# A gated delta-rule block on one core: key and query tiles by turns, decay summed in place, byte masks, shared scan banks, one joined product, and weights rounded on GpSimd

## The chip, the cores and the metric

The kernel runs on one core of a Trainium2 chip. The time is the device time of one execution in microseconds (us). Three runs of the kernel before gave 2235.35, 2230.29 and 2233.08 us, so the median is 2233.08 us.

The engines are named as the profile names them: PE (TensorE, matmuls), PEld (its weight loads), DVE (VectorE), ACT (ScalarE), POOL (GpSimd) and SP (the queue that issues nearly all DMAs). Each works through its instructions in the program's order; a scheduler fixes that order when the program is built.

## What is computed

One layer of a diffusion block over 2048 latent and 256 context tokens of width 1024. One projection feeds two branches: a gated delta rule in chunks (branch A) and a gated linear recurrence (branch B), each scanned forwards and backwards. Both are normalized, gated, projected and merged. The part of branch A that the change touches:

```python
def gdn_chunk_scan(q, k, v, g, beta, s0):
    ...
    G = jnp.cumsum(g, axis=-1)
    diff = G[..., :, None] - G[..., None, :]
    decay = jnp.where(incl, jnp.exp(jnp.where(incl, diff, 0.0)), 0.0)
    kb = k * beta[..., None]
    a_mat = jnp.where(strict, jnp.einsum('bhncd,bhnsd->bhncs', kb, k) * decay, 0.0)
    ...
    sol = lax.linalg.triangular_solve(a_mat + eye, rhs, left_side=True, lower=True,
                                      unit_diagonal=True)
    w, u = sol[..., :dk], sol[..., dk:]
    attn = jnp.einsum('bhncd,bhnsd->bhncs', q, k) * decay
    ...
    def step(S, inp):
        w_c, u_c, qg_c, attn_c, kd_c, gl_c = inp
        v_new = u_c - jnp.einsum('bhcd,bhdv->bhcv', w_c, S)
        o_c = jnp.einsum('bhcd,bhdv->bhcv', qg_c, S) + jnp.einsum('bhcs,bhsv->bhcv', attn_c, v_new)
        S = S * gl_c[..., None, None] + jnp.einsum('bhcd,bhcv->bhdv', kd_c, v_new)
        return S, o_c
```

The kernel works in chunks of 128 tokens (18 of them: 2 of context, 16 latent), with 4 heads of 128.

## The kernel before

The stages follow each other, and the scheduler lets them overlap:

1. Inputs are normalized and turned; the projections of branch A run with their convolutions; then branch B is scanned.
2. **prep** (L761) handles one chunk of branch A for both directions. It loads `l`, the chunk's keys, queries and values in one tile of one buffer. It transposes keys, queries and values (`pk`, `pq`, `pv`), sums their squares on ACT, and forms the products key by key (`pkk`, L814) and key by query (`pkq`, L822). For each direction `d` a row of log decays is loaded into `gb` (L802, two buffers), summed along the row on DVE into `dec` (L806, two buffers), put through exp on ACT (L808) and masked on POOL (L810). DVE multiplies it into `pkk` to give `an` (L817) and into `pkq` in place (L824); that result leaves through `atN` (L825). The blocks of `an` leave through `anD` and `dgD`.
3. **solve** (L837) inverts the 32x32 diagonal blocks of four chunks at once, in 62 dependent DVE instructions (L850 and L852 by turns). **levels** (L857) puts a chunk's inverse together from small PE products named `lvt`.
4. **stepA** (L959) is the scan: 18 steps in each direction, each a chain of PE products `psA`, DVE work (`r` at L991, `S` at L998) and scaled copies on ACT (L985: `vx`, `vv`, `o`).
5. The merge and the output projection end the program.

Beside stages 2 to 4 run the **gate projections**: L217, L218 and L219 by turns, 24 matmuls of 512 columns for one block of 128 output features and one group of 512 tokens. They wait for little, so the scheduler puts them between the other PE work. Below, "a filler" is one of these matmuls. Their weights come by `w_part` (L199): a DMA into `ws` (one buffer, L202), a rounding to `wh` on ACT (L203), and the remainder `wl` on POOL (L204).

In PSUM, the pool `pc` has three banks under the tag `t`, taken by turns by `pk`, `pq`, `pv`, `pkk` and `pkq`. The pool `pd` has two banks for the scan's `psA`; it is open during prep, which doesn't use it.

## Time and profile before

| what | us |
|---|---|
| median of three runs | 2233.08 |
| the profiled execution | 2233.26 |
| its span, first to last instruction | 2231.6 |

The page's part 5 groups instructions: line, engine, operation, what is written and read, count, then busy time and the mean ns of one, then the engine's idle time ahead of them and what ended it. A view of windows gives the busy time of each engine in a stretch of the span, with the number of instructions in brackets. A row of the timeline has the start and the duration, and in square brackets the idle time ahead of the instruction and what ended it. Busy times on PE are latencies that overlap: 24 fillers in a row start about 0.23 us apart and take 0.39 us each.

### The profile page before, as it was taken

What the parts mean: (1) busy time and instruction counts of PE and PEld (TensorE: products, weight loads), DVE (VectorE), ACT (ScalarE), POOL (GpSimd) and SP (SyncE); (2) the same over time, 40 slices, a digit from 0 to 9 for tenths busy, and PEclk for the clock granted to TensorE, in tenths of its full rate; (3) what the DMA queues carried; (4) which work ended last, traced back from release to release, by engine and by line L of the source; (5) the groups of instructions that cost most, each with busy time, mean ns of one, the idle gap of its engine ahead of it and who ended that gap; (6) DMA issues with size and microseconds to landing.
All of it is one profiled execution on the core that took longest, in us unless ns stands there. A gap on an engine that the chain in (4) does not pass through costs nothing. (4 is left out here: it accounts for less than half of the span.)

```text
span 2231.6 us, 40198 instructions
## 1 busy us (share of the span) xinstructions
PE 2114.9 (95%) x15056; PEld 1767.6 (79%) x15056; DVE 1404.9 (63%) x3225; ACT 925.3 (41%) x2334; POOL 688.2 (31%) x672
## 2 busy tenths in 40 slices
PE   8999999999999999999998988999989888999998
PEld 3778888888888888888776776788778877888887
DVE  4826666727776777786588788733332348766665
ACT  4623222224443444443455554344453354444441
POOL 3413433412222323234333332221133224433331
PEclk9999999999999999999999999999999999999999
DMA  9312222223323433336777778776888864444432
GB/s 340 110 35 76 64 71 77 83 76 95 106 87 100 126 95 104 101 104 195 219 224 225 255 241 214 228 231 208 236 276 278 258 228 147 145 136 127 142 95 80
DMA packets 308277, 348.15 MB, mean 156 GB/s; under 512 B 78635, under 2 KB 218161, under 8 KB 308083
## 3 DMA queue, kind: packets, MB, share of 16 engines
q1 hardware_dynamic: 306067, 338.26, 49.1%
q0 software_dynamic: 2016, 7.34, 0.9%
q8 instruction: 118, 1.93, 0.4%
q14 instruction: 76, 0.62, 0.1%
HBM read 230.46 MB, written 115.06 MB: 155 GB/s over the span
## 5 line engine op out<-in xcount | busy, mean ns | idle before, releaser
L217 PE MATMUL ps<-uhi,wh 128*128 128x512 f32 (+1 forms) x1824 | 708.2, 388 | 2.9 <-DVE uhi L306 2.6
L218 PE MATMUL ps<-ulo,wh 128*128 128x512 f32 (+1 forms) x1824 | 707.6, 388 | 3.4 <-POOL ulo L311 1.7
L219 PE MATMUL ps<-uhi,wl 128*128 128x512 f32 (+1 forms) x1824 | 705.3, 387 | 0.0
L218 PEld LDWEIGHTS ps<-ulo,wh 128*128 128x128 f32 x1824 | 345.9, 190 | 66.7 <-POOL ulo L311 2.8
L217 PEld LDWEIGHTS ps<-uhi,wh 128*128 128x128 f32 x1824 | 345.7, 190 | 66.4 <-DVE uhi L306 3.9
L219 PEld LDWEIGHTS ps<-uhi,wl 128*128 128x128 f32 x1824 | 345.6, 189 | 62.1 <-POOL wl L204 0.4
L204 POOL TENSOR_TENSOR wl<-ws,wh 128x512 fp32r<-128x512 f32 x144 | 200.2, 1391 | 551.7 <-ACT wh L203 494.4
L203 ACT CAST wh<-ws 128x512 fp32r<-128x512 f32 x144 | 89.4, 621 | 309.5 <-DMA ws<-in_w_in_dram 213.9
L419 DVE SCALAR_TENSOR_TENSOR acc<-raw,cols,acc 128x512 f32<-128x512 f32 x192 | 152.8, 848 | 0.9
L1143 PE MATMUL py<-yh,wab 128*128 128x256 f32 x512 | 145.9, 286 | 5.8 <-DVE mg L1146 5.4
L1144 PE MATMUL py<-yl,wab 128*128 128x256 f32 x512 | 145.1, 284 | 1.3 <-POOL yl L1126 1.3
L1145 PE MATMUL py<-yh,wab 128*128 128x256 f32 x512 | 144.6, 283 | 0.0
L1162 PE MATMUL pso<-uhi,mh 128*128 128x512 f32 x256 | 102.6, 402 | 7.8 <-ACT mh L1148 4.7
L605 POOL TENSOR_TENSOR bg<-s,fz 128x512 f32<-128x512 f32 (+1 forms) x36 | 37.8, 1049 | 224.9 <-ACT X L585 86.7
L1143 PEld LDWEIGHTS py<-yh,wab 128*128 128x128 f32 x512 | 97.7, 191 | 8.0 <-DVE mg L1146 6.6
L1164 PE MATMUL pso<-uhi,ml 128*128 128x512 f32 x256 | 102.2, 399 | 0.6 <-DVE ml L1149 0.6
L1163 PE MATMUL pso<-ulo,mh 128*128 128x512 f32 x256 | 101.8, 398 | 0.0
L1144 PEld LDWEIGHTS py<-yl,wab 128*128 128x128 f32 x512 | 97.7, 191 | 2.1 <-POOL yl L1126 1.7
L1145 PEld LDWEIGHTS py<-yh,wab 128*128 128x128 f32 x512 | 98.7, 193 | 0.2
L1126 POOL TENSOR_TENSOR yl<-gt,yh 128x512 fp32r<-128x512 f32 x32 | 45.0, 1408 | 148.3 <-ACT yh L1125 148.3
L998 DVE SCALAR_TENSOR_TENSOR S<-S,gl,psA 128x128 f32<-128x128 f32 x136 | 38.3, 342 | 82.5 <-PE psA L979 82.4
L1136 ACT ACTIVATE mg<-mg 128x512 f32<-128x512 f32 x64 | 40.4, 632 | 113.0 <-DMA mg<-gT 110.4
(374 smaller groups left out, 3942.3 us busy)
## 6 DMA issues: line engine op xcount, KB each, us to landing
ws<-in_w_in_dram SPq DMA_DIRECT2D x144, 256.0 KB, 3.4
gT<-gt SPq DMA_DIRECT2D x96, 256.0 KB, 3.6
kv<-knvD SPq DMA_DIRECT2D x36, 512.0 KB, 5.1
kq<-qkvD SPq DMA_DIRECT2D x32, 512.0 KB, 6.0
an<-atN SPq DMA_DIRECT2D x32, 512.0 KB, 6.2
mg<-gT SPq DMA_DIRECT2D x64, 256.0 KB, 3.4
qkvD<-acc SPq DMA_DIRECT2D x48, 256.0 KB, 2.3
l<-qkvD SPq DMA_DIRECT2D x16, 768.0 KB, 6.5
```

Of the source, the lines that this page charges most:

```text
L203: ac.copy(out=wh[:, j:j + 4, :], in_=ws)
L204: po.tensor_tensor(out=wl[:, j:j + 4, :], in0=ws, in1=wh[:, j:j + 4, :].bitcast(F32), op=ALU.subtract)
L217: te.matmul(out=ps, lhsT=wh[:, k, :], rhs=uhi[gi][:, k, :], start=(k == 0), stop=False)
L218: te.matmul(out=ps, lhsT=wh[:, k, :], rhs=ulo[gi][:, k, :], start=False, stop=False)
L219: te.matmul(out=ps, lhsT=wl[:, k, :], rhs=uhi[gi][:, k, :], start=False, stop=(k == KB - 1))
L419: ve.scalar_tensor_tensor(out=a_, in0=raw[:, o + k:o + k + n], scalar=wk, in1=a_, op0=ALU.mult, op1=ALU.add)
L1143: te.matmul(out=py[:, i, :], lhsT=wh[:, k, ms_], rhs=yh[i][:, k, :], start=(k == 0), stop=False)
L1144: te.matmul(out=py[:, i, :], lhsT=wh[:, k, ms_], rhs=yl[i][:, k, :], start=False, stop=False)
L1145: te.matmul(out=py[:, i, :], lhsT=wl[:, k, ms_], rhs=yh[i][:, k, :], start=False, stop=(k == H - 1))
L1162: te.matmul(out=ps, lhsT=mh[:, k, ts_], rhs=wout[0][k][:, ns], start=(k == 0), stop=False)
L1163: te.matmul(out=ps, lhsT=mh[:, k, ts_], rhs=wout[1][k][:, ns], start=False, stop=False)
L1164: te.matmul(out=ps, lhsT=ml[:, k, ts_], rhs=wout[0][k][:, ns], start=False, stop=(k == KB - 1))
```

## The change

- **Byte masks.** The four triangular masks are kept for the whole program as bytes (`tri8`) and no longer as five 128x128 tiles of 4 bytes a value. Where they feed a product of branch A's decays they are built again, and the tile of ones is replaced by two masks that add up to it: four more matmuls of 72 columns.
- **Keys and queries by turns.** `l` has two buffers and holds keys and queries; values have a tile of their own, `vT`.
- **Decay summed in place.** The row of log decays is loaded into `dec` itself, and the sum overwrites it; `gb` is gone. `dec` has three buffers, two of them used by each chunk.
- **Scan's banks.** `pq` and `pv` take the two banks of `pd`.
- **Joined product.** One product of the keys with keys and queries side by side (256 columns) for each head, in two banks of two heads each, in place of `pkk` and `pkq`. DVE's multiplication into the decay becomes four of 256 columns in place of two of 512.
- **Weights rounded on GpSimd.** From prep on, `wh` (80 instructions) and the weights of the merge (16) are rounded on POOL, ahead of the subtraction there.

```diff
+    tri8 = cp.tile([P, 4, P], U8, name="tri8")
...
+    with tc.tile_pool(name="tri", reuse_waits="tile", bufs=1, side="right") as tri:
+        for i, t in enumerate(tris(tri, ones)):
+            ve.tensor_copy(out=tri8[:, i, :], in_=t.bitcast(F32))
...
+    hi_ = [ac.copy]
...
-        ac.copy(out=wh[:, j:j + 4, :], in_=ws)
+        hi_[0](out=wh[:, j:j + 4, :], in_=ws)
         po.tensor_tensor(out=wl[:, j:j + 4, :], in0=ws, in1=wh[:, j:j + 4, :].bitcast(F32), op=ALU.subtract)
...
-        for masks, dst in (((m_le, m_ge), eG), ((m_gt, m_lt), erem), ((onesr, onesr), gl)):
+        for masks, dst in ((((m_le,), (m_ge,)), eG), (((m_gt,), (m_lt,)), erem), (((m_le, m_gt), (m_ge, m_lt)), gl)):
...
+    hi_[0] = po.tensor_copy
...
-            l = rc.tile([P, 3, H, P], F32, tag="l", name="l", bufs=1)
-            if lat:
-                sy.dma_start(out=l, in_=qkvD[ch])
-            else:
-                sy.dma_start(out=l[:, 0:3:2], in_=qkvD[ch, :, 0:3:2])
-            kT, qT, vT = l[:, 0], l[:, 1], l[:, 2]
+            l = rc.tile([P, 2, H, P], F32, tag="l", name="l")
+            vT = rc.tile([P, H, P], F32, tag="vT", name="vT", bufs=1)
+            sy.dma_start(out=l[:, 0:1 + lat], in_=qkvD[ch, :, 0:1 + lat])
+            sy.dma_start(out=vT, in_=qkvD[ch, :, 2])
+            kT, qT = l[:, 0], l[:, 1]
...
-                pq = pc.tile([P, H, P], F32, tag="t", name="pq", bufs=3)
+                pq = pd.tile([P, H, P], F32, tag="A", name="pq")
...
-            pv = pc.tile([P, H, P], F32, tag="t", name="pv", bufs=3)
+            pv = pd.tile([P, H, P], F32, tag="A", name="pv")
...
-                gb = rc.tile([P, H * P], F32, tag="gm", name="gb")
-                sy.dma_start(out=gb, in_=gD[d, ch].rearrange("h t -> (h t)").partition_broadcast(P))
-                dc = rc.tile([P, H, P], F32, tag="dec", name="dec")
+                dc = rc.tile([P, H, P], F32, tag="dec", name="dec", bufs=3)
+                row = dc.rearrange("p h t -> p (h t)")
+                sy.dma_start(out=row, in_=gD[d, ch].rearrange("h t -> (h t)").partition_broadcast(P))
...
+            nq = 2 if lat else 1
+            pks = [pc.tile([P, 2, 2, P], F32, tag="t", name="pkk", bufs=3) for _ in range(2)]
             for h in range(H):
-                te.matmul(out=pkk[:, h, :], lhsT=kT[:, h, :], rhs=kT[:, h, :], start=True, stop=True)
...
+                te.matmul(out=pks[h // 2][:, h % 2, 0:nq, :], lhsT=kT[:, h, :], rhs=l[:, 0:nq, h, :], start=True, stop=True)
...
-                pkq = pc.tile([P, H, P], F32, tag="t", name="pkq", bufs=3)
-                for h in range(H):
-                    te.matmul(out=pkq[:, h, :], lhsT=kT[:, h, :], rhs=qT[:, h, :], start=True, stop=True)
                 for d in range(2):
-                    ve.tensor_tensor(out=dec[d], in0=pkq, in1=dec[d], op=ALU.mult)
+                    for hh in range(2):
+                        own = dec[d][:, 2 * hh:2 * hh + 2, :]
+                        ve.tensor_tensor(out=own, in0=pks[hh][:, :, 1, :], in1=own, op=ALU.mult)
                     sy.dma_start(out=atN[ch, :, d, 0], in_=dec[d])
...
-            ac.copy(out=hi[:, k, n:n + 512], in_=ws)
+            hi_[0](out=hi[:, k, n:n + 512], in_=ws)
```

The scheduler orders the program anew. Up to the end of branch B's scan PE's order stays the same but for the four products more; the order differs from there to the end of stage 4.

**PE, in prep.** The rows below are of one latent chunk in the kernel before, ahead of and behind its two products; `ps` rows are fillers.

```order
L219 MATMUL ps<-uhi_434,wl 128x512
L814 MATMUL pkk<-l 128x128 x4
L822 MATMUL pkq<-l 128x128 x4
L217 MATMUL ps<-uhi_434,wh 128x512
L218 MATMUL ps<-ulo_435,wh 128x512
```

In the changed kernel the same place reads:

```order
L224 MATMUL ps<-ulo_333,wh 128x512
L825 MATMUL pkk<-l 128x256 x2
L225 MATMUL ps<-uhi_332,wl 128x512
L791 MATMUL pq<-ident,l 128x128 x4
L223 MATMUL ps<-uhi_332,wh 128x512
L224 MATMUL ps<-ulo_333,wh 128x512
L802 MATMUL pv<-ident,vT 128x128 x4
L825 MATMUL pkk<-l 128x256 x2
L784 MATMUL pk<-ident,l 128x128 x4
L225 MATMUL ps<-uhi_332,wl 128x512
```

The products stand in two pairs of heads with fillers and the next chunk's transposes between them; from the first chunk's products to the last chunk's, the order before has 898 fillers and the changed one 570. The fillers left over stand behind prep: the first product of the scan that waits for `r` comes after 928 and 910 fillers.

**DVE, in prep.** The rows are of the kernel before, from one chunk's `an` to the next chunk's two sums (L806).

```order
L817 SCALAR_TENSOR_TENSOR an<-pkk,nbz,dec 128x128 x8
L824 TENSOR_TENSOR dec<-pkq,dec 128x512
L830 COPY pk__10696<-an 64x4x64
L833 STREAM_TRANSPOSE dg<-an 32x128 x4
L878 COPY yt<-lvt 128x4x32
L824 TENSOR_TENSOR dec<-pkq,dec 128x512
L830 COPY pk__10696<-an 64x4x64
L806 SCALAR_TENSOR_TENSOR dec<-gb,after_9962 128x512
L806 SCALAR_TENSOR_TENSOR dec<-gb,after_9963 128x512
L885 COPY N_9955<-lvt 32x4x32 x2
```

In the changed kernel, from one chunk's last `an` on (`sT` and `sX` are solve's):

```order
L829 SCALAR_TENSOR_TENSOR an<-pkk,nbz,dec 128x128 x4
L835 TENSOR_TENSOR dec<-pkk,dec 128x256 x2
L815 SCALAR_TENSOR_TENSOR dec<-dec,after_9978 128x512
L861 TENSOR_TENSOR sT<-sA,sX 128x240
L835 TENSOR_TENSOR dec<-pkk,dec 128x256 x2
L841 COPY pk__10702<-an 64x4x64
L796 RECIPROCAL sk<-sk 128x4
L803 TENSOR_TENSOR kv<-pv,nk 128x512
L863 TENSOR_TENSOR sX<-sX,sT 128x12x20
L797 SCALAR_TENSOR_TENSOR nbz<-beta,sk 128x2x4
L861 TENSOR_TENSOR sT<-sA,sX 128x231
L799 TENSOR_TENSOR nbze<-nbz,erem 128x2x4
```

The sum of one direction now stands between the two multiplications into `dec`, and the other direction's follows some 20 rows behind the first multiplication (not shown). Between the first and the last `an`, the order before has 211 of solve's rows and the changed one 154; the rest of them now stand behind the last `an` and, all but for levels, ahead of the scan's first `r`.

**SP, in prep.** The rows are DMA issues of the kernel before, from one chunk's `atN` to the loads of `gb`. In brackets stands what an issue waits for; names with DMAHW are landings of earlier DMAs.

```order
L825 DMA atN<-dec 128x512 [waits DVE_49]
L835 DMA dgD<-dg 128x8x32 [waits DMAHW5_49,DVE_49,Activation_49]
L825 DMA atN<-dec 128x512 [waits DMAHW6_49,DVE_49]
L831 DMA anD<-pk__10429 128x384 [waits DMAHW7_49,DVE_49]
L233 DMA gT<-gt 128x512 [waits DVE_49]
L202 DMA ws<-in_w_in_dram 128x4x128 [waits DMAHW3_49,DMAHW1_49,Pool_49]
L802 DMA gb<-gD 128x512 [waits DMAHW2_49,DVE_49]
L802 DMA gb<-gD 128x512 [waits DVE_49]
L795 DMA knvD<-kv 128x1024 [waits DMAHW4_49,DVE_49,Activation_49]
```

In the changed kernel, from one chunk's `atN` to the two loads of `dec`:

```order
L836 DMA atN<-dec 128x512 [waits DVE_49]
L846 DMA dgD<-dg 128x8x32 [waits DMAHW0_49,Activation_49]
L836 DMA atN<-dec 128x512 [waits DMAHW1_49,DVE_49,Pool_49]
L842 DMA anD<-pk__10528 128x384 [waits DMAHW2_49,DVE_49]
L812 DMA dec<-gD 128x512 [waits DMAHW7_49,DMAHW3_49]
L804 DMA knvD<-kv 128x1024 [waits DMAHW4_49,DVE_49]
L239 DMA gT<-gt 128x512 [waits DMAHW5_49,DVE_49]
L812 DMA dec<-gD 128x512 [waits DMAHW6_49,DMAHW1_49]
L208 DMA ws<-in_w_in_dram 128x4x128 [waits Pool_49]
L239 DMA gT<-gt 128x512 [waits DMAHW0_49,Activation_49]
```

The load of the decay row waited for DVE's sum, which frees `gb`. It now waits for landings, among them that of the `atN` transfer out of the buffer it writes, and it stands on the queue ahead of the next loads of weights.

## The prediction

> **What bounds the kernel now.** I read the span and the busy shares first, then the busy times by stretch, then who PE waited for.

> ```profile
> span 2231.6 us, 40198 instructions
> PE 2114.9 (95%) x15056; PEld 1767.6 (79%) x15056; DVE 1404.9 (63%) x3225; ACT 925.3 (41%) x2334; POOL 688.2 (31%) x672
> ...
> core 0: us, PE busy (x) PEld busy (x) DVE busy (x) ACT busy (x) POOL busy (x), PEclk, DMA share, GB/s
> ...
> 1039.50:1179.50 140.00, 127.42 (x727) 105.78 (x725) 98.41 (x259) 70.83 (x242) 47.73 (x49) 1.00 0.75 231
> 1179.50:1359.20 179.70, 160.21 (x1307) 129.06 (x1308) 152.62 (x405) 97.67 (x334) 59.04 (x74) 0.96 0.79 240
> 1359.20:1388.00 28.80, 22.85 (x206) 18.66 (x204) 23.40 (x64) 8.13 (x28) 5.29 (x6) 0.99 0.68 167
> 1388.00:1797.90 409.90, 382.09 (x3368) 329.26 (x3369) 160.82 (x485) 179.55 (x569) 99.10 (x113) 0.98 0.79 246
> 1797.90:2231.60 433.70, 406.90 (x2530) 360.52 (x2529) 274.36 (x452) 175.59 (x476) 143.44 (x97) 0.98 0.42 134
> ```

> PE is busy 95% of the span. Its work hardly changes, so the time can move only by PE's idle time. The first two windows are prep, from the first chunk's `pkk` to the eighth's (1179.5) and to the last one's (1359.2): 319.7 us, PE busy 287.6, idle 32.1. The third runs to the scan's first `r` product, the fourth is the rest of the scan, the last the merge, whose code doesn't change but for who rounds its weights. In prep DVE is busy 251.0 us, 79%.

> ```profile
> PE psA L979 <- ACT vx L985: 12.5, 8, 2.9
> PE pkk L814 <- ACT kv L778: 9.2, 9, 1.5
> PE pkq L822 <- ACT junk L784: 8.0, 9, 2.8
> PE psA L979 <- DVE r L991: 7.8, 2, 4.9
> PE pkq L822 <- DVE kv L794: 6.1, 5, 1.7
> PE pk L775 <- DMA l<-qkvD: 5.5, 4, 1.9
> ```

> Columns are the total in us, the number of waits and the longest. The waits of `pkk`, `pkq` and `pk` sum to 28.8 us, most of prep's 32.1. The first two products wait for a bank: with three banks by turns, `pkk` needs the one that `pk` held until ACT had copied it, `pkq` that of `pq` or `pv`. `pk` waits for the load into the single buffer of `l`.

> **What the change removes.** With `pq` and `pv` in the scan's two banks, and `l` in two buffers, each of these four waits loses its cause: a bank's last reader is then a chunk back. At best 28.8 us go. But PE follows others here, so I ask what is late next.

> **What prep's work becomes.** Fillers cost this much:

> ```profile
> 1041.99 0.39 PE L217 MATMUL ps<-uhi,wh 128*128 128x512 f32 x1
> ...
> 1047.43 0.39 PE L217 MATMUL ps<-uhi,wh 128*128 128x512 f32 x1
> ```

> These starts lie 24 fillers apart: 5.44 / 24 = 0.227 us each. The order has 898 of them in prep before and 570 now. PE's work in prep falls by 328 x 0.227 = 74.5, to 287.6 - 74.5 = 213.1 us. This work isn't saved; it is done later.

> DVE's work falls less:

> ```profile
> L806 DVE TENSOR_TENSOR_SCAN dec<-gb,after 128x512 f32<-128x512 f32 x36 | 47.6, 1324 | 37.9 <-DMA atN<-dec 22.6 <-issue 9.4 <-DMA gb<-gD 5.1
> L850 DVE TENSOR_TENSOR sT<-sA,sX 128x31 f32<-128x31 f32 (+25 forms) x155 | 60.1, 388 | 12.9 <-DMA sA<-dgD 9.3
> L852 DVE TENSOR_TENSOR sX<-sX,sT 128x31 f32<-128x31 f32 (+25 forms) x155 | 61.3, 395 | 3.5
> L824 DVE TENSOR_TENSOR dec<-pkq,dec 128x512 f32<-128x512 f32 x32 | 21.9, 685 | 1.8 <-PE pkq L822 1.4
> L543 DVE TENSOR_TENSOR sn<-ps,s 128x256 f32<-128x256 f32 x8 | 3.3, 419 | 0.1
> ```

> Solve's rows between the first and the last `an` fall from 211 to 154: 57 x 0.39 = 22 us. The multiplication into the decay goes from two of 0.685 us in a chunk to four of 256 columns; L543, also out of PSUM, gives 0.42 us, so 16 x (4 x 0.42 - 2 x 0.685) adds 5. That leaves some 234 us on DVE against 213 on PE. **DVE becomes the fuller engine**, and PE can't run ahead of it: a chunk's products need the banks that DVE frees with the last chunk's `an` and multiplications.

> **What the change adds: a loop through two transfers.** The row L806 has it in the making: the sum already waited 22.6 us for `atN` to leave its buffer, with the next row of decays waiting in `gb`. Now the row can only be fetched once `atN` has left. Three buffers for two uses a chunk mean that one direction's sum in each chunk writes the buffer of the other direction in the chunk before. These are the times to landing, minimum, median and maximum, of `gb` and of `atN` out of `dec`:

> ```profile
> DMA to landing us min/median/max: 3.0/3.9/5.3
> ...
> DMA to landing us min/median/max: 4.2/5.0/7.8
> ```

> ```profile
> L817 DVE SCALAR_TENSOR_TENSOR an<-pkk,nbz,dec 128x128 f32<-128x128 f32 x144 | 39.7, 342 | 0.2
> L808 ACT ACTIVATE dec<-dec 128x512 f32<-128x512 f32 x36 | 22.8, 632 | 65.8 <-DVE dec L806 65.6
> L810 POOL TENSOR_SCALAR_AFFINE_SELECT dec<-dec 128x512 f32<-128x512 f32 x36 | 30.5, 848 | 61.9 <-ACT dec L808 59.9 <-issue 1.9
> ```

> From one chunk's multiplications to the next one's: 2 x 0.42, then `atN` out 5.0, the row in 3.9, the sum 1.32, exp 0.63, mask 0.85, four `an` 1.37: 13.9 us, and 14 with the two issues. On SP the load of `dec` waits for that landing, and the next loads of `ws`, `l` and `vT` are queued behind it; on DVE all that stands behind the sum waits. In the stretch before solve begins DVE has less than this to do, so the loop sets the pace there; later DVE's own work is about as long.

> *First part (8 chunks).* DVE's 98.4 less 24 of solve's 57 rows (9 us) is 89, or 11 a chunk. The two context chunks have no `atN`, so 2 x 11 + 6 x 14 = 106 us. *Second part (10 chunks).* DVE's 152.6 less 33 rows (13 us), with 3 more for the multiplications, is 143: 14.3 a chunk, beside a loop of 14. Two limits of one length seldom fall in step, and I add 0.3: 146 us. Prep is then 252 us long, 68 shorter than before, but PE has only 213 of work in it. Its idle time is 39 us against 32.1: **+7**. Bounds: with DVE never waiting, 234 - 213 = 21 us idle, -11; with both landings at their longest (13.1 in place of 8.9) 67 us more.

> **From prep to the scan's first `r`.** The third window has 28.8 - 22.85 = 5.95 us of idle PE. It and one later wait come from DVE, which stood still for solve and for `sqt`:

> ```profile
> 1387.00 0.20 DVE L933 TENSOR_SCALAR sqt<-sqt 128x64 f32<-128x64 f32 x1 [4.45 <-DMA sqt<-sqD]
> ...
> 1388.04 1.23 PE L979 MATMUL psA<-r,an 128*128 128x128 f32 x4 [4.92 <-DVE r L991]
> ...
> 1411.81 0.20 DVE L850 TENSOR_TENSOR sT<-sA,sX 64x31 f32<-64x31 f32 x1 [4.74 <-DMA sA<-dgD]
> ...
> 1413.58 0.64 PE L979 MATMUL psA<-r,an 128*128 128x128 f32 x3 [2.93 <-DVE r L991]
> ```

> In the new order all of solve and `sqt` stand ahead of the first `r`, with 340 fillers (77 us of PE) between prep's end and it. DVE has 310 - 154 = 156 solve rows left there, 61 us. PE is the longer one, so both waits go: **-6** and **-3**. If DVE is late by more than these 16 us, they stay.

> **The joined product.** Here the two products follow each other:

> ```profile
> 1066.46 1.05 PE L814 MATMUL pkk<-l 128*128 128x128 f32 x8
> 1067.35 1.06 PE L822 MATMUL pkq<-l 128*128 128x128 f32 x8
> 1068.16 0.48 PE L218 MATMUL ps<-ulo,wh 128*128 128x512 f32 x1
> ...
> L331 PE MATMUL pm<-stgl,sc 128*2 128x512 f32 x32 | 14.1, 592 | 0.0
> L814 PE MATMUL pkk<-l 128*128 128x128 f32 x144 | 20.4, 285 | 9.2 <-ACT kv L778 9.2
> ```

> 16 records take 1.70 us, 0.106 each. A joined one costs between that (0.85 a chunk saved, 14 us in all) and twice that (nothing). In 4-byte products 384 more columns cost 592 - 285 = 307 ns, so 128 more cost 0.10, as much as a record of their own: I take **0**.

> **The rest.** ACT loses 96 casts; it is busy 44% of the scan (179.55 of 409.90), and its `vx` waits (12.5 us) arise where no filler stands between `r` and `vx`. Such places are 7 before and 10 now, while the fillers reach further into the steps that had none; I take 0, within -8 to +10. Masks and the four matmuls of 72 columns lie beside a full stretch of fillers: under 1 us.

> The rounding on POOL has its price in this:

> ```profile
> 1361.62 1.49 POOL L204 TENSOR_TENSOR wl<-ws,wh 128x512 fp32r<-128x512 f32 x1
> ...
> 1361.90 1.24 DVE L790 TENSOR_TENSOR nbze<-nbz,erem 128x8 f32<-128x8 f32 x1
> ...
> L790 DVE TENSOR_TENSOR nbze<-nbz,erem x18: 153/166/1237, 1043.0 to 1361.9; 128x8 f32<-128x8 f32 x18
> L755 POOL CAST after<-m_lt 128x512 uint8<-128x512 f32 x1 | 0.6, 611 | 0.0
> ```

> An instruction of 8 elements, 0.17 us in the median, took 1.24 beside POOL's subtraction. A cast of 512 columns takes POOL 0.61 us, as long as on ACT, so the weights come no later. 570 / 24 = 24 casts in prep could hold DVE between 0 and 24 x 0.61 = 15 us; the masking (L810), also with one input, shows no such wait of DVE among the rows above, so I take 0 and keep the other end. [...]

> **The sum.** The profiled execution took 2233.3 us, 1.7 beyond its span and 0.2 beyond the median. 2233.3 + 7 - 6 - 3 + 0 = **2231 us**, no change (a measurement here can tell about 0.2%, 4.5 us, from none).

> **Rivals.**
> *The loop runs short (faster).* With landings at their shortest, 7.2 us, the loop is 12.2: 22 + 6 x 12.2 + 143 = 238 us, 25 idle, -7 in place of +7: 2217. A fuller scan could give 5 more. For it: the moved fillers and weights thin the traffic of prep. Against: prep's other bytes come in four fifths of the time, and the DMA share was 0.79 already.
> *The loop runs long (slower).* If the two landings need 1.6 us more in each of 16 chunks, prep is 26 us longer: 2257. It decides from the point where they exceed 8.9 us together; SP, held by the load's wait, makes them likely to be issued late as well.
> *The casts hold DVE (slower).* DVE sets the second part, and half of its bound, 8 us, lands on the sum: 2239.
> *The waits are only renamed:* that PE idles as much behind DVE as behind ACT is what the forecast says already.

> **How the numbers follow.** The forecast has 0.45, with a range of its own of 2222 to 2240; it splits into faster 0.15, same 0.20, slower 0.10. The short loop 0.27, nearly all faster; the long loop 0.20 and the casts 0.08, slower but for 0.03. That makes faster 0.41, same 0.24, slower 0.35. The range runs to 2203, the short loop with the products' and the scan's gain, and to 2262, the long loop with a part of the casts.

> **What would show it.** Right: prep some 250 us long with PE idle near 39 us, its products waiting for DVE (`an` or `dec`); DVE's sum waiting for the load of `dec` by several us a chunk in the first eight; no wait of `r` on solve. Wrong: prep's PE idle under 25 us (DVE or the loop is shorter) or over 55 (landings); the time moving in the scan or the merge, for which I expect nothing.

## The result, and the profile after

The changed kernel took 2269.94 us (median of four, 2268.52 to 2274.66), the kernel before 2231.68 in the same session: a ratio of 1.0163, with a 95% interval of 1.0143 to 1.0184. By the ratio the change makes it 36 us slower (38 by the medians). The forecast was 2231, its range ended at 2262. The profiled execution took 2268.52 us.

The page of the changed kernel begins like this:

```profile
span 2266.8 us, 40030 instructions
PE 2131.5 (94%) x14932; PEld 1767.8 (78%) x14932; DVE 1408.2 (62%) x3258; ACT 877.6 (39%) x2238; POOL 757.1 (33%) x773
```

PE is busy for 16.6 us longer, with 124 instructions fewer. Nearly all of its work is the same (the fillers all remain, and the joined rows are busy for 40.3 us, the two products before for 20.4 and 21.1), so its instructions ran slower. The windows show where. The edges are the first `pkk`, that of the ninth chunk (1179.5 in the kernel before, which the prediction calls the eighth's), the last one, the scan's first `r` product, the end of the last step, and the end:

```profile
core 0: us, PE busy (x) PEld busy (x) DVE busy (x) ACT busy (x) POOL busy (x), PEclk, DMA share, GB/s
1036.20:1137.70 101.50, 87.20 (x412) 68.90 (x410) 84.63 (x223) 55.89 (x211) 41.23 (x43) 0.97 0.81 241
1137.70:1300.70 163.00, 134.04 (x1049) 102.00 (x1049) 141.41 (x400) 88.11 (x317) 61.90 (x85) 0.91 0.81 243
...
1300.70:1431.50 130.80, 105.72 (x911) 81.93 (x909) 92.63 (x233) 26.57 (x65) 38.31 (x53) 0.86 0.55 153
1431.50:1831.20 399.70, 380.65 (x3094) 328.82 (x3093) 127.32 (x388) 140.47 (x490) 127.32 (x153) 0.99 0.77 242
1831.20:2266.80 435.60, 407.33 (x2534) 360.83 (x2533) 275.97 (x452) 175.77 (x477) 144.90 (x97) 0.98 0.42 133
```

In the kernel before, the first `r` product starts at 1370.0; the 1388.0 of the prediction is the next one, of the other direction. With that edge its windows are:

```profile
core 0: us, PE busy (x) PEld busy (x) DVE busy (x) ACT busy (x) POOL busy (x), PEclk, DMA share, GB/s
1039.50:1359.20 319.70, 287.62 (x2034) 234.84 (x2033) 251.02 (x663) 168.50 (x575) 106.77 (x123) 0.98 0.77 236
1359.20:1370.00 10.80, 9.74 (x83) 8.10 (x82) 10.57 (x30) 4.86 (x18) 3.92 (x5) 1.00 0.86 190
1370.00:1797.90 427.90, 395.20 (x3493) 339.83 (x3492) 173.64 (x519) 182.82 (x579) 100.47 (x114) 0.98 0.78 242
```

From the first `pkk` to the first `r` the kernel before takes 319.7 + 10.8 = 330.5 us, the changed one 101.5 + 163.0 + 130.8 = 395.3: **64.8 us more**. The scan gives 28.2 back (427.9 to 399.7), the merge costs 1.9 and the start gives 3.3; that is the 35.2 us between the spans.

The 64.8 us have three parts. PE's idle time in that stretch goes from 32.1 + 1.1 = 33.2 to 14.3 + 29.0 + 25.1 = 68.4 us, +35. PE's work at full clock goes from 291 to 298, as some levels moved there from the scan (1104 of their products stand ahead of `r`, 704 before). The rest, 23 us, is the clock: it falls to 0.91 and 0.86. By the trace's clock records PE is busy for 58.7 us at half clock there, where fillers start 0.43 us apart in place of 0.227; so half of that, 29.3 us, is lost, against 6.4 before. The prediction had no term for that.

The waits of PE in that stretch (total in us, times, longest):

```profile
PE pkk L825 <- DVE dec L835: 10.2, 8, 2.9
PE ps L223 <- POOL wh L209: 8.2, 5, 4.1
PE pkk L825 <- ACT kv L787: 7.3, 4, 3.6
PE lvt L893 <- DVE yt L889: 6.5, 3, 4.7
PE pq L791 <- DMA l<-qkvD: 5.3, 5, 1.8
PE lvt L899 <- DVE N L896: 4.6, 4, 2.3
PE lvt L911 <- DVE yt L908: 4.3, 3, 2.6
```

The four waits that the change was to end have not all gone. `pkk` still waits 7.3 us for `kv` (9.2 before; each of the four ends some 0.05 us behind the end of that copy), and 5.3 us go to the load of `l`, now under `pq` (5.5 under `pk`). Only the two of `pkq` shrank, from 14.1 to 6.2 us under `pq` and `pv`. New are the others: the products wait for VectorE's multiplications, the fillers for weights cast on POOL, the levels for VectorE's copies. The longest shows how they come about. VectorE first, then PE and, in the last row, the queue SP:

```profile
1306.24 0.67 DVE L238 COPY gt<-ps 128x512 f32<-128x512 f32 x1
1306.84 0.40 DVE L863 TENSOR_TENSOR sX<-sX,sT 128x247 f32<-128x247 f32 x1
1308.35 1.23 DVE L815 TENSOR_TENSOR_SCAN dec<-dec,after 128x512 f32<-128x512 f32 x1 [1.11 <-DMA dec<-gD]
1309.49 0.40 DVE L861 TENSOR_TENSOR sT<-sA,sX 128x252 f32<-128x252 f32 x1
1309.92 0.42 DVE L863 TENSOR_TENSOR sX<-sX,sT 128x252 f32<-128x252 f32 x1
1310.38 0.89 DVE L861 TENSOR_TENSOR sT<-sA,sX 128x255 f32<-128x255 f32 x1
1311.19 0.28 DVE L889 COPY yt<-lvt 128x128 f32<-128x128 f32 x1
```

```profile
1306.04 0.39 PE L225 MATMUL ps<-uhi,wl 128*128 128x512 f32 x1
1306.36 0.45 PE L887 MATMUL lvt<-n,an 32*32 32x32 f32 x32
1311.52 0.64 PE L893 MATMUL lvt<-yt,n 32*32 32x32 f32 x16 [4.71 <-DVE yt L889]
...
1325.74 0.79 PE L223 MATMUL ps<-uhi,wh 128*128 128x512 f32 x1 [1.03 <-POOL wh L209]
...
1320.49 0.46 SPq L208 DMA_DIRECT2D ws<-in_w_in_dram  x1
```

PE's first product of a level is done at 1306.8. Its copy stands on VectorE behind a sum that waits for its row, and behind solve's rows, and starts at 1311.19. In PE's order no filler stands beside these products: the last one starts at 1306.04, the next at 1325.74, and that one waits for its weights. SP issued their load at 1320.49, 35.8 us after the load before it (1284.70), with 37 other transfers between, 16 of them loads of `sqt`. So PE stands still for 4.71 us here, and for 13.4 us in all from 1306.8 to 1325.7. In windows of 10 us, PE then pays a second time:

```profile
1300.00:1310.00 10.00, 6.81 (x72) 5.16 (x72) 7.34 (x21) 2.10 (x7) 0.00 (x0) 0.97 0.71 186
1310.00:1320.00 10.00, 3.52 (x80) 2.88 (x80) 9.40 (x27) 5.04 (x17) 2.04 (x5) 0.50 0.54 122
1320.00:1330.00 10.00, 6.21 (x103) 4.68 (x104) 9.35 (x28) 2.75 (x10) 2.83 (x6) 0.50 0.76 201
1330.00:1340.00 10.00, 10.00 (x62) 7.75 (x64) 2.89 (x8) 2.78 (x3) 3.91 (x7) 1.00 0.54 171
```

For 20 us the granted clock is 0.50, and for 10.3 of them (20 less 3.52 and 6.21) PE is idle as well.

### The profile page after: what moved, and what is told of

It is laid out like the page before. It is cut to its first block, busy times and chain, and to the rows that moved or that the text cites. A ratio compares the mean times of both kernels' runs of the same rounds, so it can differ in the third digit from the quotient of the medians.

```text
span 2266.8 us, 40030 instructions
## 1 busy us (share of the span) xinstructions
PE 2131.5 (94%) x14932; PEld 1767.8 (78%) x14932; DVE 1408.2 (62%) x3258; ACT 877.6 (39%) x2238; POOL 757.1 (33%) x773
## 5 line engine op out<-in xcount | busy, mean ns | idle before, releaser
L210 POOL TENSOR_TENSOR wl<-ws,wh 128x512 fp32r<-128x512 f32 x144 | 209.0, 1451 | 258.8 <-ACT wh L209 248.7
L209 POOL CAST wh<-ws 128x512 fp32r<-128x512 f32 x80 | 51.2, 640 | 223.8 <-DMA ws<-in_w_in_dram 150.6
L1174 PE MATMUL pso<-ulo,mh 128*128 128x512 f32 x256 | 101.5, 397 | 0.0
L209 ACT CAST wh<-ws 128x512 fp32r<-128x512 f32 x64 | 39.7, 620 | 148.7 <-DMA ws<-in_w_in_dram 99.0
```

What stands on the lines that cost most here:

```text
L209: hi_[0](out=wh[:, j:j + 4, :], in_=ws)
L210: po.tensor_tensor(out=wl[:, j:j + 4, :], in0=ws, in1=wh[:, j:j + 4, :].bitcast(F32), op=ALU.subtract)
L1174: te.matmul(out=ps, lhsT=mh[:, k, ts_], rhs=wout[1][k][:, ns], start=False, stop=False)
```

## The experiments

Each kernel was timed beside the kernel before, so ratios to it are compared, with 95% intervals. Three theories stood at the start. **Theory 1, the order:** with the banks free, prep's chunks stand closer together, the fillers leave prep, and what is on VectorE can't keep up with the order. **Theory 2, the loop:** the sum in place fetches its row only when `atN` has left. **Theory 3, the casts:** rounding on POOL holds VectorE and the weights. "u_" kernels are the changed kernel with something undone or added, "b_" kernels the kernel before with something done. From each one's order: fillers between first and last `pkk`, and how many of solve's 310 rows stand ahead of the first `r`. From its profile: PE idle, and PE's busy time lost to half clock, both from the first `pkk` to the first `r` or the last `pkk`, whichever is later, in us.

| kernel | ratio (interval) | fillers | rows | idle | half clock |
|---|---|---|---|---|---|
| before | 1 | 898 | 212 | 33 | 6 |
| changed | 1.0163 (1.0143-1.0184) | 570 | 310 | 68 | 29 |
| b_bank: banks alone | 1.0099 (1.0083-1.0115) | 652 | 248 | 41 | 17 |
| b_join: joined product alone | 1.0044 (1.0030-1.0058) | 957 | 199 | 31 | 5 |
| b_act: casts on POOL alone | 0.9977 (0.9966-0.9987) | 900 | 216 | 36 | 14 |
| b_dec: sum in place alone | 1.0087 (1.0074-1.0101) | 900 | 215 | 43 | 16 |
| b_dec2: the same, four tiles | 1.0082 (1.0068-1.0095) | 898 | 209 | 40 | 15 |
| u_act: casts on ACT | 1.0085 (1.0068-1.0102) | 687 | 273 | 48 | 17 |
| u_gb1: row in its own buffer | 1.0071 (1.0048-1.0094) | 709 | 263 | 51 | 18 |
| u_bank: pq, pv in three banks | 1.0141 (1.0117-1.0166) | 634 | 310 | 61 | 32 |
| u_join: products apart | 1.0142 (1.0115-1.0168) | 494 | 310 | 66 | 26 |
| u_mix2: fillers named in prep | 1.0082 (1.0052-1.0112) | 734 | 248 | 54 | 18 |
| u_hold: late solve held | 1.0096 (1.0072-1.0121) | 570 | 186 | 49 | 22 |
| u_hold0: same, not held | 1.0110 (1.0074-1.0147) | 570 | 291 | 59 | 19 |
| u_act_hold | 1.0071 (1.0043-1.0099) | 687 | 186 | 43 | 9 |
| b_act_hold | 0.9995 (0.9980-1.0011) | 899 | 189 | 35 | 8 |
| u_pace: fillers by data, 770 | 1.0142 (1.0117-1.0168) | 770 | 282 | 72 | 24 |
| u_pace3: the same, 905 | 1.0104 (1.0084-1.0124) | 905 | 211 | 51 | 20 |
| u_pace3_act: and casts on ACT | 1.0081 (1.0059-1.0102) | 910 | 212 | 45 | 14 |
| u_pace3_gb1: and own buffer | 1.0029 (1.0012-1.0045) | 895 | 215 | 42 | 14 |

**One part alone, from the kernel before.** The banks:

```diff
-                pq = pc.tile([P, H, P], F32, tag="t", name="pq", bufs=3)
+                pq = pd.tile([P, H, P], F32, tag="A", name="pq")
...
-            pv = pc.tile([P, H, P], F32, tag="t", name="pv", bufs=3)
+            pv = pd.tile([P, H, P], F32, tag="A", name="pv")
```

> The kernel before with one part of the change: pq and pv in the scan's two banks. Its order has 652 fillers between the first and the last pkk (before 898, changed kernel 570). Theory 1 (prep emptied of fillers: PE's work goes, the waits behind DVE and for loads stay, PE stands idle and its clock falls to half; then the rest of solve and the levels wait once more behind prep): slower, 2245 to 2260, granted clock over the span under 0.98. Theory 2 (the loop through the decay buffer in place): gb is still separate here, so no slower than before, 2220 to 2235. Theory 3 (casts on POOL hold DVE and the weights): the casts are still on ACT, 2220 to 2235.

It took 2254.5 us, as theory 1 has it. Its prep, to the first `r`, and its scan:

```profile
1041.50:1301.30 259.80, 226.49 (x1534) 189.21 (x1533) 223.44 (x574) 147.87 (x519) 86.51 (x98) 0.95 0.83 255
1301.30:1389.60 88.30, 80.54 (x587) 62.75 (x586) 61.79 (x160) 27.85 (x74) 22.73 (x31) 0.94 0.58 154
1389.60:1822.80 433.20, 404.19 (x3495) 349.01 (x3487) 157.94 (x477) 181.23 (x576) 98.86 (x112) 0.95 0.75 234
```

Two free banks shorten prep by 60 us and make the kernel 22 us slower, with neither loop nor casts. In the profiled execution (2260.1 us, the longest of the four) the idle time up to `r` is only 8 us above before; what is lost is the granted clock, 0.94 to 0.95 in all three windows.

The joined product alone (L814 and L822 replaced as in the change):

> The kernel before with the joined product alone (two banks of pkk and pkq columns). Its order has 957 fillers in prep. Theory 1: prep is no emptier, so 2225 to 2240. Price of the joined product itself: between 0 and -14 us in PE busy. Theories 2 and 3: no change either.

2242.1 us, ratio 1.0044: above what I expected. Idle time and half clock up to `r` are as before and larger behind it, in code that it doesn't touch. The joined rows keep PE busy for 41.8 us, the two products apart for 20.4 and 21.1, so the product saves nothing there. Why the rest was worse was not followed up.

The casts alone (`hi_[0] = po.tensor_copy` from prep on, as in the change):

> The kernel before with the weights rounded on POOL from prep on, alone; 900 fillers in prep. Theory 3: slower by 10 to 25 us, fillers wait for wh, DVE's instructions longer. Theories 1 and 2: no change, 2228 to 2238.

2227.2 us: a little faster, the reverse of theory 3 in this order. It was the fastest of all.

**The casts undone in the changed kernel.**

```diff
-    hi_[0] = po.tensor_copy
```

> The changed kernel with the weights rounded on ACT again; 687 fillers in prep (570 with POOL). Theory 3: most of the 38 us comes back, 2232 to 2242. Theory 1: a part, as the order is half way back, 2245 to 2262. Theory 2: the loop is still there, 2260 to 2275.

2251.2 us, in the middle, as theory 1 said; but its order moved too (687 fillers). So I took the order and each part in turn.

**The order alone.** In the changed kernel two groups of fillers are named behind each chunk; the data waits are the same:

```diff
+            for _ in range(2):
+                next(rest, None)
...
-    for i in range(24 - NLATE, 24):
-        gate_block(i, (0, 1))
+    for _ in rest:
+        pass
```

> The changed kernel with nothing undone; only the program names two groups of fillers behind each chunk of prep, ahead of the next one, so that they stand in prep: 734 fillers between the first and the last pkk (changed kernel 570), 186 of solve's 310 rows (154). Theory 1 (prep emptied of fillers, then solve and the levels alone, and the halved clock behind each longer pause): a good part comes back, 2240 to 2255, with less idle time and less lost clock. Theory 2 (loop through the decay buffer) and theory 3 (casts on POOL): all of it is still there, 2262 to 2278.

2250.9 us, where theory 1 said. Half of the loss hung on where the fillers stand, and on what moves with them (248 of solve's rows ahead of `r`, not 310), with every part of the change in place.

**Row, products and banks undone in the changed kernel, one at a time.** For the first:

```diff
-                dc = rc.tile([P, H, P], F32, tag="dec", name="dec", bufs=3)
+                gb = rc.tile([P, H * P], F32, tag="gm", name="gb", bufs=1)
+                dc = rc.tile([P, H, P], F32, tag="dec", name="dec", bufs=2)
```

> The changed kernel with the row of decays in a buffer of its own again (one, and two of dec: the same three tiles), so that the row's load waits no longer for atN to leave. 709 fillers in prep. Theory 2: the sum's waits for the load go, and with them most of the 38 us, 2235 to 2250. Theory 1: a part comes back because prep is fuller, 2245 to 2262. Theory 3: 2262 to 2275. To tell 1 from 2, the sum's waits in the trace of the changed kernel must be as large as the loss.

> The changed kernel with pkk and pkq apart again. 494 fillers in prep, 119 of solve's rows: emptier than the changed kernel's (570, 154). Theory 1: no faster, 2265 to 2285, though the product itself may give some us back. Theories 2 and 3: 2262 to 2275. If the joined product is what costs (the kernel before with it alone was 10 us slower): 2255 to 2262.

> The changed kernel with pq and pv in prep's own three banks again. 634 fillers in prep, 173 of solve's rows. Theory 1: between, 2250 to 2265. If the banks are the one cause: 2240 to 2250. Theories 2 and 3: 2262 to 2275.

The row gave back 20 us (2249.9, which theories 1 and 2 both allow), the other two about 5 (2264.4, 2264.8), inside the intervals. Banks that cost 22 us alone give 5 when undone: chunks stand close together without them (634 fillers), which I put down to `l` in two tiles. No run undoes that, or the byte masks. The parts don't add up; each is also a new order.

**Solve's place.** Up to here the time went with the number of solve's rows ahead of `r`: 310 rows, 2264 to 2270; 248 to 273, 2250 to 2255; 199 to 216, 2227 to 2242. That made **theory 4**: rows moved from the scan, where VectorE has room, to a place where it has none. The test holds solve's last two groups until a late filler's copy `late` exists:

```diff
-            po.memset(Xf, 0.0)
+            if late is None:
+                po.memset(Xf, 0.0)
+            else:
+                for i in range(2):
+                    po.tensor_scalar(out=Xf[:, 512 * i:512 * i + 512], in0=late, scalar1=0.0, scalar2=None, op0=ALU.mult)
```

> The changed kernel with nothing undone, but solve's last two groups (chunks 12 to 17 of prep's order, 124 of 310 rows) held until the last filler ahead of the scan has left PSUM. Its order has 570 fillers in prep and the first r product at filler 905, both as in the changed kernel (570, 910), but 186 of solve's rows ahead of r where the changed kernel has 310 and the kernel before 212. Theory 4 (what costs is that VectorE's solve rows were moved from the scan, where VectorE has room, to a place ahead of the first r, where it is the fuller engine): r comes up to 124 x 0.42 = 52 us earlier, the rows hide in the scan, 2225 to 2250. Theory 1 (an empty prep costs by itself): 2260 to 2275, as prep is as empty as in the changed kernel. Theory 2 (loop through the decay buffer) and 3 (casts): 2260 to 2275.

> The same program without the wait: solve's last two groups come behind the fillers in the program, but nothing holds them. 570 fillers in prep, r at filler 905, 291 of solve's rows ahead of r. Theory 4: nearly all of the loss is back, 2255 to 2272, and at least 10 us above the kernel with the wait. Theories 1 to 3: the same time as with the wait, within 5 us.

> The changed kernel with the weights rounded on ACT again and solve's last two groups held: 687 fillers in prep, 186 rows ahead of r (without the wait 273, 2251 us). Theory 4: 87 rows fewer, 2228 to 2242. Theory 1: unchanged, 2246 to 2256. Theory 3: the casts on POOL cost 19 us in the changed kernel, and as many beside the held solve: this one is 15 to 20 us faster than the held one with the casts on POOL; by theory 4 within 10 us of it.

> The kernel before with the weights rounded on POOL (2227 us) and solve's last two groups held: 189 rows ahead of r instead of 216, 899 fillers in prep. Theory 4: 27 rows x 0.42 = 11 us less for VectorE ahead of r, but PE is the fuller engine there in this kernel: 2218 to 2230. If holding solve costs something of its own (levels late in the scan): 2230 to 2240.

Theory 4 falls: 186 rows ahead of `r` (2256.1 us) or 291 (2258.9) make no difference that the intervals could tell. Both are, by their ratios, 12 to 15 us better than the changed kernel (the interval of the second just touches its own), which theories 1 to 3 didn't expect of the first either: they had 2260 to 2275. So the number of fillers in prep, 570 in all three, isn't what counts by itself. What the two share is that the fillers are named ahead of the last levels; I read it as their place, which no run shows alone. With the casts on ACT the held kernel (2250.7) is 5 us faster, inside the intervals, and the kernel before with casts on POOL gains nothing by holding (2234.4).

One thing in the traces goes with the time better than the counts do. In the four slowest kernels, changed, u_pace, u_bank and u_join (2264 to 2270), PE's order has a stretch of 19 to 21 us without a filler soon behind the last `pkk`, and PE is idle for 12 to 15 us of it. In the other sixteen the longest such stretch is 11 us, with at most 7.5 idle. The loads of weights ahead of it left SP 30 to 41 us apart in these four; up to `r`, they do so at most 29.6 us apart in the others. No run moved that load alone, so that the queue SP set this place is not shown.

**The old spread of fillers, forced.** Each chunk's load of `l` waits for the copies of fillers named behind the chunk ahead of it:

```diff
+            for _ in range(2 + (pos % 3 == 2)):
+                next(rest, None)
...
+            if pos:
+                ac.copy(out=l[:, 0, 0, 0:1], in_=lastg[0][:, 0:1])
```

> The changed kernel with nothing undone; each chunk's load of keys and queries waits until the two or three groups of fillers named behind the chunk before it have left PSUM. Its order has 905 fillers between the first and the last pkk, r at filler 910 and 211 of solve's rows ahead of r: all three as in the kernel before (898, 928, 212; changed kernel 570, 910, 310). Theory 1 (the loss comes from an order that packs prep: the same work stands between the first chunk and the first r, but VectorE's chunks, solve and the levels are no longer spread over it): the 38 us come back, 2222 to 2242, idle and lost clock between the first pkk and the first r 40 to 50 us (changed kernel 98, before 40). Theory 2 (loop through the decay buffer) and theory 3 (casts on POOL): both are still there; 2250 to 2270.

> The same with the weights rounded on ACT: 910 fillers in prep, 212 rows ahead of r. Theory 1: 2225 to 2245, within 8 us of the one with the casts on POOL, and, as in the kernel before, rather slower than faster than it. Theory 3: 15 us or more faster than it.

> The same as the first, always with two groups a chunk: 770 fillers in prep, 282 rows ahead of r, between the changed kernel and the kernel before. Theory 1: between their times, 2240 to 2258. Theories 2 and 3: 2255 to 2272.

With 905 fillers in prep and `r` where it was, the kernel still took 2257.5 us: only a third of the loss is back (1.0163 to 1.0104), where theory 1 alone had all of it. What is left is seen in its waits:

```profile
PE ps L223 <- DVE gt L240: 30.3, 11, 5.2
PE ps L223 <- ACT gt L238: 6.9, 4, 4.3
```

Fillers wait for copies of earlier fillers, which stand in VectorE's queue with the sums, and the sums waited this long for the loads of their rows (us, times):

```profile
  DMA dec<-gD: 38.7, 21
```

With two groups always (770 fillers) the same wait bought nothing: 2267.0, again above theory 1's range. Casts on ACT gave 5.7 us, inside the intervals.

**The loop alone.** So the sum in place was made in the kernel before and nothing else. By the counts the order stays (900 fillers, `r` at 930); row by row it is a new one, with 1921 of PE's 2034 rows in prep and 545 of VectorE's 664 still in sequence:

```diff
-                gb = rc.tile([P, H * P], F32, tag="gm", name="gb")
-                dc = rc.tile([P, H, P], F32, tag="dec", name="dec")
+                dc = rc.tile([P, H, P], F32, tag="dec", name="dec", bufs=3)
+                gb = dc.rearrange("p h t -> p (h t)")
```

> The kernel before with the sum in place alone: the row of decays is loaded into dec (three tiles), gb is gone, nothing else. Its order is that of the kernel before: 900 fillers in prep, r at filler 930, 215 of solve's rows ahead of r (898, 928, 212). Theory 2 (VectorE stands still before the sum, for a row that is fetched only once atN has left, and all that is queued behind it waits, copies of fillers among it): slower, 2243 to 2260; the sum's waits become waits for the load of dec, above 35 us in all, and PE waits for gt. Theory 1 (order) and 3 (casts): 2228 to 2238.

> The same with four tiles of dec, the bytes that gb and dec took together before: 898 fillers in prep, r at filler 928, 209 rows ahead of r. A tile's row may then be fetched a chunk earlier. Theory 2, by the loop's length: the loop is half as tight, 2226 to 2240, and 8 us or more below the one with three tiles. If the sum in place costs for another reason: as slow as with three tiles, within 5 us.

2253.2 us: 19 us for the sum in place with the order that came of it. The casts alone (b_act) moved as many rows (1897 and 548 still in sequence) and made the kernel 5 us faster, so a reshuffle of this size need not cost; it isn't excluded. What the sum waited for, in this kernel (us, times; before, it waited 22.6 for `atN`, 9.4 and 5.1), and its prep and scan:

```profile
  DMA dec<-gD: 43.1, 19
  issue: 2.9, 1
```

```profile
1036.50:1373.70 337.20, 297.74 (x2039) 242.47 (x2037) 259.06 (x666) 171.29 (x585) 108.73 (x127) 0.95 0.75 225
...
1387.60:1815.50 427.90, 398.87 (x3475) 344.06 (x3475) 171.19 (x509) 184.29 (x579) 100.66 (x114) 0.96 0.77 240
```

The sum's waits grew by 9 us in all (37.1 to 46.0). Prep is 17.5 us longer: 7.4 of idle PE (39.5 against 32.1), and most of the rest is the clock, 0.95 against 0.98. The waits of PE for `gt` that theory 2 expected are not in it; up to `r` the levels' products wait 11.9 us there, 3.7 before. The row has lost its lead: from its issue to the start of its sum passed 18.5 us before (median of 36), and 4.8 here. A row and its sum in the kernel before, then in this one:

```profile
1099.53 0.32 SPq L802 DMA_DIRECT2D gb<-gD  x1
...
1117.45 1.72 DVE L806 TENSOR_TENSOR_SCAN dec<-gb,after 128x512 f32<-128x512 f32 x1
```

```profile
1200.26 0.40 SPq L803 DMA_DIRECT2D dec<-gD  x1
...
1204.52 1.23 DVE L806 TENSOR_TENSOR_SCAN dec<-dec,after 128x512 f32<-128x512 f32 x1 [1.11 <-DMA dec<-gD]
```

A fourth tile, which I expected to loosen the loop, gave nothing (2252.1; issue to sum 5.1 us): the row is still issued just ahead of its sum. So a tile more doesn't bring the lead back. Why the order makes no use of the fourth stays open.

**Both together:** the old spread of fillers, and the row in its own buffer.

> The changed kernel with the spread of fillers of the kernel before, as in the run with 905 fillers in prep (2257.5), and the row in a buffer of its own again (one gb, two of dec): 895 fillers in prep, r at filler 936, 215 rows ahead of r. Theory 2: 15 us or more come back, 2228 to 2243, and PE's waits for gt (37 us there) fall under 20. Theory 3 (casts): 2250 to 2260, as the casts are still on POOL.

2240.0 us, ratio 1.0029 against 1.0104: 17 us back, as theory 2 said, and PE's waits for the copies of fillers shrink to these:

```profile
PE ps L223 <- DVE gt L240: 7.9, 4, 4.1
PE ps L223 <- ACT gt L238: 6.4, 4, 1.9
```

With the spread and the loop undone 30 of the 36 us are back, while banks, joined product, casts, masks and the two tiles of `l` stay: together they cost some 6 us in this order (3 to 10 by the interval). In its profile PE waits 16.9 us for loads of `l` (4.6 in u_pace3), which the forced spread holds; what the 6 us are was not traced further. That one `gb` suffices there is shown by the time, not explained: its rows have no more lead than in the changed kernel (6.0 us in both, 6.9 in u_gb1, 5.2 in u_pace3), and the sums still wait 32.5 us, against 38.7. So the lost lead goes with the cost in b_dec, but it is not shown to be the cause of it.

## Why the prediction was wrong

**The sign is wrong, and the step that failed is the one from prep to the scan's first `r`:** "PE is the longer one, so both waits go: -6 and -3." I had compared two totals, 77 us of fillers against 61 of solve's rows, and taken the larger as the length. Both were short: measured, PE has 93 us of work at full clock there, with the levels, and VectorE 92.6, of which solve's rows are 72.1. But the stretch lasts 130.8 us, so neither is the bound. The levels pass from PE to VectorE, to ACT and back, their place among the fillers is fixed, and each engine waits for the other in turn: PE is idle for 25.1 us in place of the 1.1 of the kernel before, and the granted clock is 0.86. More than half of the idle time, 13.4 us, lies in the 19 us without a filler, whose weights were loaded late; the prediction took the 340 fillers as work that is always at hand. Of the 58 us of idle time and half clock that came on top up to `r` (35 and 23), 36 arise there: 25.1 idle and 12.3 of busy time lost to half clock, less 1.1 before.

**No term for the clock.** The prediction said that PE's work hardly changes, so that only its idle time could move the time. The work didn't change (2086 us at full clock before, 2088 after, the clock's loss taken off), but PE lost 43.8 us of busy time to half clock instead of 28.9. In prep 11.2 us more of idle time came with 10.6 us more of half clock.

**Prep, by its own steps.** "Each of these four waits loses its cause" held for a third: 18.8 of the 28.8 us are still there, in part under other names. Why a bank's last reader is not a chunk back for `pkk`, as forecast, the record doesn't show. First part, 106 us: measured 101.5. Second part, 146: measured 163.0, with VectorE busy for 141.4 (I had 143). So VectorE's work was right and "two limits of one length seldom fall in step, and I add 0.3" a chunk was far too little: it was 2.2 a chunk, over the nine steps that this part has (the prediction counted ten). Prep took 264.5 us against 252, its idle time was 43.3 against 39. The products waited for VectorE (`dec`), as forecast. That the sum would wait by several us a chunk for its row didn't show in the changed kernel: 13.0 us in all. That the sum in place costs was seen in other kernels (19 us in the kernel before, 17 with the old spread), not in the sum's own waits here.

**The other terms.** The joined product: 0; for PE's work that is right (41.8 us against 41.5 in b_join), and undoing it gave 5 us, within the intervals (1.0142 against 1.0163), but alone it made the kernel 10 us slower. The scan: "0, within -8 to +10"; it became 28.2 us shorter, with 14.6 us less of PE's busy time, as levels had left it, and 13.7 less of idle time. The casts: 0, with up to 15; the kernel before became 5 us faster by them. Beside them solve's rows did take longer:

```profile
L861 DVE TENSOR_TENSOR sT<-sA,sX 128x31 f32<-128x31 f32 (+25 forms) x155 | 66.8, 431 | 19.6 <-DMA sA<-dgD 15.9
L863 DVE TENSOR_TENSOR sX<-sX,sT 128x31 f32<-128x31 f32 (+25 forms) x155 | 64.4, 415 | 3.6
```

They are 388 and 395 ns before, 391 and 406 with the casts back on ACT: with the casts on POOL VectorE is busy for 7.7 us longer with them. That lies between the 15 us that the prediction kept as its upper end and nothing; what lengthens the rows the traces don't show, and it did not set the time.

**The rivals.** The long loop (2257, by 26 us of later landings) came nearest in time, and the sum in place did cost 19 us, but not as priced: the two landings together were not later, medians of 5.2 us for the row and 2.8 for `atN` in the changed kernel against 3.9 and 5.0 (of the few landings that the traces have, 5 and 9 against 12 and 6). "The waits are only renamed" was set aside as part of the forecast; it was half of the truth, since some kept their name and the new ones came in larger pieces, which cost more than they last (up to `r`, 23 us of half clock came with 35 of idle time).

## What to carry to other kernels

Where a scheduler sets one order for engines that take their work in turn, more buffers are also a new order. Ask what it takes out from behind the waits, whether the filling work has its data by then, and price the stretch by its chains, not by the larger of two totals. A load that fills its own tile early may be worth its bytes: loading into the tile that the last use must leave first saved a buffer here and cost the lead. And look at the granted clock of each stage first, and sum PE's idle time over short windows: in these traces a window of 3.41 us at full clock with 2.0 us or more of idle PE was followed by one at half clock in 216 of 216 cases, one with less than 1.25 us in 25 of some 11,850.

## What the runs showed of the hardware

```profile
1340.33 0.50 PE L224 MATMUL ps<-ulo,wh 128*128 128x512 f32 x1
1340.66 0.40 PE L225 MATMUL ps<-uhi,wl 128*128 128x512 f32 x1
1345.13 0.77 PE L223 MATMUL ps<-uhi,wh 128*128 128x512 f32 x1 [4.07 <-POOL wh L209]
1345.69 0.63 PE L224 MATMUL ps<-ulo,wh 128*128 128x512 f32 x1
1346.12 0.63 PE L225 MATMUL ps<-uhi,wl 128*128 128x512 f32 x1
```

After the pause fillers start 0.43 us apart, in place of 0.227: the pause of 4.1 us is followed by a stretch at half speed to about 1350, some 2.5 us more. The clock records have half clock from 1343.6 to 1350.5 there. These are counts and times of this case's executions; why the clock falls and returns, no trace here shows.
